# Product "4" of two pairs ahead of the first weight sums, and casts of weights bound behind snapshots on ScalarE

## The chip, the cores and the metric

The kernel runs on one core of a Trainium2 chip, as one program. The time is the device time of one execution, in microseconds (us); the median of several runs counts.

The engines of the core each run their own instructions in the order in which they were written down for them, and wait for one another by semaphores: TensorE (matmuls, called PE in the profile), VectorE (DVE), ScalarE (ACT), GpSimd (POOL) and SyncE (SP). SP, ScalarE and GpSimd issue DMAs; in this kernel GpSimd issues those that add to what is in memory already.

## The reference

A trunk of two layers works on 512 tokens of 1024 channels, with 16 learned tokens put ahead (528 in all). Each layer is a feed-forward block (FFN), a mixer (linear attention and softmax attention, merged by gates), and another FFN:

```
def swiglu(x, w_gate, w_up, w_down):
    return (jax.nn.silu(x @ w_gate) * (x @ w_up)) @ w_down
...
    for l in range(DEPTH):
        h = h + 0.5 * swiglu(rmsnorm(h, norm_gains[l, 0]),
                             ffn_w_gate[l, 0], ffn_w_up[l, 0], ffn_w_down[l, 0])
        h = h + mixer(rmsnorm(h, norm_gains[l, 1]), ...)
        h = h + 0.5 * swiglu(rmsnorm(h, norm_gains[l, 2]),
                             ffn_w_gate[l, 1], ffn_w_up[l, 1], ffn_w_down[l, 1])
    return rmsnorm(h, final_norm)[:, N_META:]
```

`rmsnorm` divides by the root of the mean square over the 1024 channels and multiplies by a gain. The inner width of an FFN is 2816, that is 22 tiles of 128, and everything is float32.

## The kernel before

**Layout.** The state `h` stays on chip, channels on the 128 partitions in 8 chunks (`KC`), 528 tokens along the row. A norm's gain is multiplied into the operand before the matmuls, and its factor 1/root(mean square), `rs`, afterwards, so the matmuls can begin before `rs` is known.

**Precision.** Every matmul runs in a rounded float32 and is done three times: operands and weights are split into a high and a low part, and high x high, high x low and low x high are added in PSUM. A block of weights, 128 x 1024 float32 (512 KB), is loaded into one of three buffers; ScalarE casts it to its high part (`whi`, L227) and VectorE subtracts that to get the low part (`wlo`, L228). Each kind has four buffers. `Weights.make` issues cast and subtraction in the order of the program's plan, some 3 or 4 blocks ahead of the product that uses them, and `Weights.fetch` the loads some 6 ahead.

**The FFN's gate and up projections.** 22 tiles make 11 pairs. For a pair the four products of a 2 x 2 block of weights with a 2 x 2 block of the operand (the tokens are cut in two halves, the channels in two halves) are replaced by seven, after Strassen and Winograd; their names are "1" to "7" and their order within a pair is mostly 1 2 5 6 7 4 3 or close to it. Products "1", "2" and "4" use the blocks 11, 12 and 22 of the weights as they are (`DIRECT`). Products "6", "7", "5" and "3" use sums of blocks, which no engine computes: s3 and s4 begin as the negative of a block on ScalarE (`negative`, L178), s1 and s2 as a load on SP, and a DMA on GpSimd's queue adds the other block in memory (`add`, L183). A product is 24 matmuls of 128 x 128 weights by up to 264 tokens (L517).

**Accumulators.** "1", "6", "7" and "4" of a pair add up in one PSUM tile (X), "5" and "3" in another (Z), "2" has its own (Y). Between two of them ScalarE copies the sum so far out of PSUM, the "snapshot" (L523): p1 after "1", q after "6", r after "7". The next product into that tile waits for the snapshot. VectorE adds these to the results `c`, and `hidden` makes silu(gate) x up of a tile, with `rs` multiplied in. `hidden(st, p, 1)` reads product "4"'s result in PSUM, so it takes the tile in two cuts.

**The order of steps.** `ffn_steps` writes an FFN's order out: `("P", pair, product)` and `("D", ...)` for pieces of the down projection, in three groups of 4, 4 and 3 pairs. The first group opens with 1 and 2 of pairs 0 and 1, then 6 and 5 of pair 0, 7, 4, 3, and so on. `weight_plan` makes the order of weights from the same list. After product "5" of pair 0 the kernel calls `norm.rs()`: the squares (L427) have been added by VectorE (L431); two pairs of matmuls with a constant sum them over the partitions (`means`, L399), ScalarE takes logarithm (L405) and exponential (L376) and a last square (L409), and VectorE makes a Newton step. These run at high priority. The scheduler of the framework puts each engine's instructions in order by priority and readiness; `after(x)` makes the instructions issued within it stay behind `x` on their engine, and `act` keeps ScalarE's functions in order in this way and notes the last of them in `prev_act`.

**The end.** The last FFN's down projection for the last three chunks (`LATE` = 5 to 7) is done for one half of the tokens and then for the other (`ending`). The final norm's factor is made for each half; `leave` multiplies two chunks of h by it (L1067) and sends them out (L1068). The first half leaves while the second half's chunks are computed.

## Time and profile before

| what | value |
| --- | --- |
| median of 3 runs | 2239.12 us (2236.11 to 2239.44) |
| the profiled execution | 2237.59 us |
| its span (first to last instruction) | 2235.8 us |
| TensorE matmul busy | 2197.9 us, 98% |
| VectorE / ScalarE / GpSimd busy | 68% / 54% / 7% |
| mean DMA rate over the span | 141 GB/s |

A line of a timeline has the start in us from the span's start, the duration, engine, source line, operation, output<-input by the program's names, shapes and a count; in brackets stands how long the engine had been idle before it and what ended that. "ss", "s2", "mm" are PSUM tiles, "xc" the FFN's operand, "t" a scratch tile. ACTq, POOLq and SPq stand for DMAs issued by these engines. Matmuls overlap: one is shown with 0.28 us, but the next begins 0.12 us after it.

### The profile page before, as it was taken

The page shows a single profiled execution, that of the slowest core. Times are in us where ns is not written, and L with a number is a line of the kernel's source. Part 1 is how long each engine was busy: PE and PEld are TensorE (multiplying, and loading weights), DVE is VectorE, ACT ScalarE, POOL GpSimd, SP SyncE. Part 2 cuts the span into 40 slices and gives each one's busy share as a digit, 9 for nine tenths or more (in the row PEclk, how much of TensorE's full clock was granted, in tenths as well). Part 3 has the DMA queues.
Part 4 walks back from the last instruction along what each step waited for, and adds up shares of the span by engine and source line. Part 5 has one row for each costly group of instructions (what it writes and reads, how often), then busy time and mean ns, then how long its engine had stood idle before and what let it go on. Part 6 is the DMA issues. An engine that isn't in the chain of part 4 may idle for free.

```text
span 2235.8 us, 39768 instructions
## 1 busy us (share of the span) xinstructions
PE 2197.9 (98%) x16506; PEld 2093.8 (94%) x16506; DVE 1521.6 (68%) x2415; ACT 1196.6 (54%) x1769; POOL 154.1 (7%) x180
## 2 busy tenths in 40 slices
PE   7999999999999999999999999999999999999998
PEld 6999999989999999999999999999788888989897
DVE  7657567586986676565696575675878767756566
ACT  7536355454785574453575363553457836636353
POOL 1111010000000010101011110100000001101010
PEclk9999999999999999999999999999999999999999
DMA  9769563212113485866667685632121136859671
GB/s 265 211 156 225 143 170 102 84 48 77 48 39 109 127 211 156 192 179 171 176 172 199 166 215 141 176 100 76 53 80 48 48 123 167 221 150 217 161 179 66
DMA packets 88612, 315.57 MB, mean 141 GB/s; under 512 B 9840, under 2 KB 12272, under 8 KB 88432
## 3 DMA queue, kind: packets, MB, share of 16 engines
q1 hardware_dynamic: 61136, 218.26, 29.1%
q0 software_dynamic: 25344, 92.29, 23.3%
q8 instruction: 129, 2.11, 0.4%
q10 hardware_dynamic: 1952, 2.50, 0.3%
q14 instruction: 51, 0.42, 0.1%
HBM read 264.77 MB, written 2.10 MB: 119 GB/s over the span
## 4 chain that ended last, share of the span: by engine, by line
PE 86%; DVE 6%; ACT 4%; DMA 3%; issue 1%; DVEq 0%; POOL 0%; ACTq 0%; POOLq 0%
PE ss L517 37%; PE ss L393 27%; PE mm L393 13%; PE sm L393 2%; DMA w<-win 2%; DVE wlo L228 1%; PE sm L894 1%; PE ss L869 1%; ACT whi L227 1%; ACT t L376 1%; PE sm L910 1%; PE sm L911 1%; PE ss L870 1%; PE ss L399 1%; PE sm L719 0%
## 5 line engine op out<-in xcount | busy, mean ns | idle before, releaser
L517 PE MATMUL ss<-xc,whi 128*128 128x264 f32 (+1 forms) x4928 | 903.9, 285 | 16.4 <-ACT whi L227 9.5
L517 PEld LDWEIGHTS ss<-xc,whi 128*128 128x128 f32 x4928 | 767.1, 189 | 20.0 <-ACT whi L227 9.7
L517 PE MATMUL ss<-xc,wlo 128*128 128x264 f32 (+1 forms) x2464 | 702.1, 285 | 2.7 <-DVE wlo L228 2.7
L393 PE MATMUL ss<-g,whi 128*128 128x264 f32 (+2 forms) x2692 | 495.4, 300 | 0.0
L517 PEld LDWEIGHTS ss<-xc,wlo 128*128 128x128 f32 x2464 | 466.0, 189 | 5.0 <-DVE wlo L228 4.7
L393 PEld LDWEIGHTS ss<-g,whi 128*128 128x128 f32 x2692 | 391.4, 188 | 16.2
L393 PE MATMUL mm<-x,whi 128*128 128x264 f32 (+1 forms) x1712 | 384.8, 315 | 0.0
L227 ACT CAST whi<-w 128x1024 fp32r<-128x1024 f32 (+1 forms) x221 | 230.7, 1046 | 259.8 <-PE ss L393 117.0
L227 ACT CAST whi<-raw 128x1024 fp32r<-128x1024 f32 x190 | 199.3, 1049 | 293.7 <-PE mm L393 97.9
L228 DVE TENSOR_TENSOR wlo<-w,whi 128x1024 fp32r<-128x1024 f32 (+1 forms) x221 | 267.7, 1218 | 107.8 <-ACT whi L227 106.0
L393 PE MATMUL ss<-g,wlo 128*128 128x264 f32 (+2 forms) x1346 | 312.2, 300 | 0.0
L228 DVE TENSOR_TENSOR wlo<-raw,whi 128x1024 fp32r<-128x1024 f32 x190 | 232.1, 1222 | 96.1 <-ACT whi L227 94.7
L393 PEld LDWEIGHTS mm<-x,whi 128*128 128x128 f32 x1712 | 278.4, 188 | 16.6 <-issue 1.0
L393 PE MATMUL mm<-x,wlo 128*128 128x264 f32 (+1 forms) x856 | 266.1, 315 | 0.0
L393 PEld LDWEIGHTS ss<-g,wlo 128*128 128x128 f32 x1346 | 215.7, 188 | 8.3
L228 DVE TENSOR_TENSOR wlo<-s,whi 128x1024 fp32r<-128x1024 f32 x88 | 107.6, 1223 | 97.1 <-ACT whi L227 97.0
L227 ACT CAST whi<-s 128x1024 fp32r<-128x1024 f32 x88 | 92.4, 1050 | 146.7 <-PE ss L517 127.1
L393 PEld LDWEIGHTS mm<-x,wlo 128*128 128x128 f32 x856 | 159.6, 188 | 8.5 <-issue 0.7
L483 DVE SCALAR_TENSOR_TENSOR t<-ss,rs 128x528 f32<-128x528 f32 (+1 forms) x93 | 64.5, 700 | 127.1 <-PE ss L393 127.0
L178 ACT ACTIVATE s<-w 128x1024 f32<-128x1024 f32 x88 | 93.2, 1060 | 75.5 <-DMA w<-win 41.3
L183 POOL DMA_DIRECT2D w<-win x44 | 38.9, 884 | 944.5 <-DMA w<-win 430.3
L523 ACT COPY snap<-ss 128x528 f32<-128x528 f32 (+1 forms) x132 | 77.1, 584 | 0.9 <-PE ss L517 0.9
(245 smaller groups left out, 2566.8 us busy)
## 6 DMA issues: line engine op xcount, KB each, us to landing
w<-win SPq DMA_DIRECT2D x219, 512.0 KB, 4.6
raw<-wts SPq DMA_DIRECT2D x190, 512.0 KB, 3.3
s<-win POOLq DMA_DIRECT2D x44, 512.0 KB, 7.3
w<-s POOLq DMA_DIRECT2D x44, 512.0 KB, 5.5
w<-win POOLq DMA_DIRECT2D x44, 512.0 KB, 7.0
s<-w POOLq DMA_DIRECT2D x44, 512.0 KB, 7.3
h<-xt SPq DMA_DIRECT2D x3, 528.0 KB, 6.4
out<-h ACTq DMA_DIRECT2D x4, 256.0 KB, 2.3
```

Of the source, the lines that this page charges most:

```text
L178: self.nc.scalar.activation(t, w, AF.Copy, scale=-1.0)
L183: self.nc.gpsimd.dma_start(t, src, accum_op=ALU.add)
L227: nc.scalar.copy(hi[:, cs], w[:, cs])
L228: nc.vector.tensor_tensor(lo[:, cs], w[:, cs], hi[:, cs].bitcast(F32), ALU.subtract)
L376: prev_act[0] = S.activation(*args, **kw).ins
L393: TE.matmul(acc.half[i][:width], lhs, rhs[:, acc.spans[i]], start=first, stop=last)
L399: TE.matmul(a, weights, x[:, hs], start=True, stop=True)
L483: V.scalar_tensor_tensor(cut(dst[rows]), pv[rows], -0.5 * f, cut(rs[rows]), ALU.mult, ALU.mult)
L517: TE.matmul(acc[:, j], a[:, j, k], b[:, at], start=bool(begin and k == 0 and i == 0), stop=k == len(x) - 1 and i == 2, skip_group_check=no ...
L523: S.copy(st[name], acc)
L869: TE.matmul(s[:n, i, :HF], lhs, kh[:, hs], start=True, stop=False)
L870: TE.matmul(s[:n, i, :HF], lhs, kl[:, hs], start=False, stop=True)
```

## The change

1. In the very first FFN (layer 0, first block) the order of steps opens with products 1, 2 of pairs 0 and 1 and then product "4" of both pairs; "6" and "5" of pair 0 follow. The loads of the plan move with them. Such an early "4" gets a PSUM tile of its own (W), ScalarE copies it to `c`, and after product "7" VectorE adds the snapshot r to it and calls `hidden` in one cut.
2. `Weights.make` issues its casts and the start of its sums under `issue_after(W.behind)`. `W.behind` is the last snapshot of pairs 0 and 1, in every FFN, and after `norm.rs()` it is the norm's last square, which is now issued through `act`. For later pairs it is None.
3. In `ending` all four `leave` of the first half come after the last chunk's add of the second half, and no longer between its chunks.

The arithmetic is the same but for the order in which r and product "4" are added in pairs 0 and 1 of the first FFN.

```diff
 DIRECT = {"1": "11", "2": "12", "4": "22"}
-def ffn_steps():
+def ffn_steps(opening):
     steps, pair = [], 0
...
         ahead = g == 0
         steps += [("P", p, c) for p in range(pair, pair + 1 + ahead) for c in "12"]
+        early4 = (0, 1) if opening and ahead else ()
+        steps += [("P", p, "4") for p in early4]
         steps += [("P", pair, c) for c in "65"]
         for i in range(n):
             p, more = pair + i, i + 1 < n
...
                 [[("D", g, 0, 0, 2 * n - 2)], [("D", g, 1, 0, 2 * n - 2)]]
             if ahead and i == 0:
                 early = [[], []]
-            steps += early[0] + [("P", p, "7")] + early[1] + [("P", p, "4"), ("P", p, "3")]
+            steps += early[0] + [("P", p, "7")] + early[1] + [("P", p, c) for c in "43" if c == "3" or p not in early4]
             if more:
                 steps += [("P", p + 1, "6"), ("P", p + 1, "5")]
         steps += [("D", g, m, 0, 2 * n - 2) for m in range(2, HELD)]
...
             plan.append(("tile", name, idx, k * P, col, width))
     def ffn(l, f):
-        for step in ffn_steps():
+        for step in ffn_steps((l, f) == (0, 0)):
             if step[0] == "P":
                 plan.append(("op", (l, f)) + step[1:])
             else:
...
         self.at = {load: i for i, load in enumerate(self.loads)}
         self.made, self.fetched, self.got, self.summed, self.raws = 0, 0, {}, {}, {}
         self.pos = 0
+        self.behind = None
     def dram(self, f, i, name):
         return self.win[((f[0] * 2 + f[1]) * NPAIR + i) * 4 + ("11", "12", "21", "22").index(name)]
...
             self.fetched += 1
     def make(self, upto):
+        with self.tc.issue_after(self.behind) if self.behind else nullcontext():
+            self.make_all(upto)
+    def make_all(self, upto):
         nc = self.nc
         while self.made < min(upto, len(self.loads)):
             self.fetch(self.made + 1)
...
         act(y, y, AF.Exp, scale=-0.5)
         if newton:
             u = slot("t", n=y.shape[-1])
-            S.activation(u, y, AF.Square)
+            act(u, y, AF.Square)
             V.scalar_tensor_tensor(cut(u), ms, EPS, cut(u), ALU.add, ALU.mult)
             V.scalar_tensor_tensor(y, u, 3.0, y, ALU.subtract, ALU.mult)
...
         def product_of_pair(p, product):
             kind = "s2" if p % 2 == 0 else "ss"
             st = made.setdefault(p, {})
+            apart = product == "4" and "r" not in st
             where, begin = {"1": ("X", 1), "6": ("X", 0), "7": ("X", 0), "4": ("X", 0), "2": ("Y", 1), "5": ("Z", 1),
                             "3": ("Z", 0)}[product]
+            if apart:
+                where, begin = "W", 1
             if begin:
                 st[where] = pair(kind == "s2")
             acc = st[where][:, :, :w]
...
             def snapshot(name):
                 t = slots["snap"].tile([P, T], F32, tag="snap", name=nm("snap"))[:, :n]
                 st[name] = v2(t)
-                S.copy(st[name], acc)
+                copied = S.copy(st[name], acc).ins
+                W.behind = copied if p < 2 else None
             if product == "1":
                 snapshot("p1")
...
                 V.tensor_tensor(st["c"][:, :, 0], st["p1"], acc, ALU.add)
             elif product == "6":
                 snapshot("q")
+            elif apart:
+                S.copy(st["c"][:, :, 2], acc)
+                st["apart"] = True
             elif product == "7":
                 snapshot("r")
                 V.tensor_tensor(st["c"][:, :, 3], st["r"], st["Z"][:, :, :w], ALU.add)
+                if "apart" in st:
+                    V.tensor_tensor(st["c"][:, :, 2], st["c"][:, :, 2], st["r"], ALU.add)
+                    hidden(st, p, 1)
             elif product == "4":
                 hidden(st, p, 1)
             elif product == "3":
...
             c = st["c"]
             t, u = [c[:, j, 2 * m : 2 * m + 2].rearrange("p q c -> p (q c)") for j in range(2)]
             x21 = st["X"][:, :, :w]
-            cuts = [(t, u, t, u, slice(0, n))] if m == 0 else \
+            cuts = [(t, u, t, u, slice(0, n))] if m == 0 or "apart" in st else \
                 [(t[:, :w], u[:, :w], x21[:, 0], x21[:, 1], slice(0, w)), (t[:, w:], u[:, w:], t[:, w:], u[:, w:], slice(w, n))]
             for td, _, ts, _, cs in cuts:
                 V.scalar_tensor_tensor(td, ts, -0.5, rs[:, cs], ALU.mult, ALU.mult)
...
             if g == len(GROUPS) - 1:
                 (done or finish_chunk)(m)
-        steps = ffn_steps()
+        steps = ffn_steps((l, f) == (0, 0))
         last_op = max(i for i, t in enumerate(steps) if t[0] == "P")
         for i, step in enumerate(steps):
             if step[0] == "P":
...
                 product_of_pair(*step[1:])
                 if step[1:] == (0, "5"):
                     rs = norm.rs()
+                    W.behind = prev_act[0]
                 if i == last_op:
                     close_pools(norm.pools)
                     following()
...
             product("ffn_w_down", acc, operand, len(w), only=i, w=w)
             t, sq[i] = slot("t")[:, hs[i]], slot("t")[:, hs[i]]
             V.scalar_tensor_tensor(t, acc.half[i], -0.25, rs[:, hs[i]], ALU.mult, ALU.mult)
-            V.tensor_tensor(h(c, hs[i]), h(c, hs[i]), t, ALU.add)
+            added = V.tensor_tensor(h(c, hs[i]), h(c, hs[i]), t, ALU.add).ins
             if c == KC - 1:
                 ms[i] = pair()[:, 0, : SEQ // 2]
                 TE.matmul(ms[i], o1024, fin.acc[:, hs[i]], start=True, stop=False)
...
             else:
                 TE.matmul(ms[i], o1024, sq[i], start=False, stop=True)
             gain(c, hs[i])
+            return added
         def factor(i):
             y[i], u = slot("t")[:, hs[i]], sq[i]
...
             chunk(0, c)
         factor(0)
         chunk(1, LATE)
-        leave(0, (0, 2))
         for c in range(LATE + 1, KC):
-            chunk(1, c)
-        leave(0, (4, 6))
+            added = chunk(1, c)
+        with after(added):
+            leave(0, (0, 2, 4, 6))
         factor(1)
         leave(1, (0, 2, 4, 6))
```

More of the change, by code (lines that the diff above doesn't have):

```diff
@@ L148, with __init__ @@
 class Weights:
-    def __init__(self, nc, raw, hi, lo, wts, win):
-        self.nc, self.raw, self.hi_pool, self.lo_pool, self.wts, self.win = nc, raw, hi, lo, wts, win
+    def __init__(self, tc, raw, hi, lo, wts, win):
+        nc = tc.nc
+        self.tc, self.nc, self.raw, self.hi_pool, self.lo_pool, self.wts, self.win = tc, nc, raw, hi, lo, wts, win
         self.long = self.short = None
@@ L277, in build @@
     small = pool("small", 4)
-    W = Weights(nc, pool("wraw", 3), pool("whi", 4), pool("wlo", 4), wts, win)
+    W = Weights(tc, pool("wraw", 3), pool("whi", 4), pool("wlo", 4), wts, win)
     pss = pool("pss", 2, bass.MemoryType.PSUM)
```

## The prediction

> **What bounds the kernel now.** I read the page first: its parts 1 and 5 for the engine that sets the time, then the windows of the start, then the timelines of the places where that engine stood idle.
>
> ```profile
> span 2235.8 us, 39768 instructions
> PE 2197.9 (98%) x16506; PEld 2093.8 (94%) x16506; DVE 1521.6 (68%) x2415; ACT 1196.6 (54%) x1769; POOL 154.1 (7%) x180
> ...
> L517 PE MATMUL ss<-xc,whi 128*128 128x264 f32 (+1 forms) x4928 | 903.9, 285 | 16.4 <-ACT whi L227 9.5
> L517 PE MATMUL ss<-xc,wlo 128*128 128x264 f32 (+1 forms) x2464 | 702.1, 285 | 2.7 <-DVE wlo L228 2.7
> ```
>
> TensorE is busy for 98% of the span. The number of matmuls doesn't change, so a change of order can only touch what is left: 2235.8 - 2197.9 = 37.9 us of idle time, and matmuls that ran at a lowered clock. Of the idle time 16.4 + 2.7 us stand ahead of the products of the gate and up projections (L517), where the edit works. The windows say where.
>
> ```profile
> 0.00:50.00 50.00, 34.60 (x208) 31.58 (x209) 36.93 (x63) 39.21 (x62) 8.25 (x13) 0.97 0.94 258
> 50.00:100.00 50.00, 50.00 (x413) 50.00 (x412) 36.79 (x47) 32.24 (x40) 6.95 (x8) 1.00 0.91 245
> ...
> 35.00:40.00 5.00, 3.75 (x28) 3.44 (x27) 4.69 (x6) 2.93 (x4) 1.73 (x2) 1.00 1.00 245
> 40.00:45.00 5.00, 1.54 (x9) 1.10 (x8) 2.09 (x4) 3.32 (x5) 0.88 (x1) 0.97 0.98 225
> 45.00:50.00 5.00, 5.00 (x32) 5.00 (x31) 3.23 (x5) 3.05 (x3) 0.88 (x1) 0.69 0.62 104
> ```
>
> The columns are the window, then TensorE matmul, weight load, VectorE, ScalarE and GpSimd busy with counts, then granted clock, DMA share and GB/s. In the first 50 us TensorE lacks 15.4 us; in the next 50 it lacks none, and 413 matmuls in 50 us give 0.121 us each, 2.9 us for a product of 24. So 35 to 50 us is the place to look at, and the DMA engines are full there until 45 us.
>
> ```profile
> 26.21 0.39 PE L517 MATMUL ss<-xc,wlo 128*128 128x264 f32 x1 [0.26 <-DVE wlo L228]
> 37.98 1.13 PE L399 MATMUL ss<-t,const 128*128 128x264 f32 x4 [1.25 <-issue]
> 42.55 0.52 PE L517 MATMUL ss<-xc,whi 128*128 128x264 f32 x2 [2.22 <-ACT whi L227]
> 44.31 0.51 PE L517 MATMUL ss<-xc,whi 128*128 128x264 f32 x2 [1.25 <-ACT snap L523]
> 46.16 0.64 PE L517 MATMUL ss<-xc,whi 128*128 128x264 f32 x2
> 46.82 0.64 PE L517 MATMUL ss<-xc,whi 128*128 128x264 f32 x2
> 48.13 0.41 PE L517 MATMUL ss<-xc,whi 128*128 128x264 f32 x2
> 48.51 0.40 PE L517 MATMUL ss<-xc,whi 128*128 128x264 f32 x2
> ...
> 24.53 0.59 ACT L523 COPY snap<-ss 128x528 f32<-128x528 f32 x1
> 35.41 0.64 ACT L427 ACTIVATE t<-h 128x528 f32<-128x528 f32 x1
> 41.45 1.04 ACT L227 CAST whi<-w 128x1024 fp32r<-128x1024 f32 x1 [3.52 <-DMA w<-s]
> 43.68 0.58 ACT L523 COPY snap<-ss 128x528 f32<-128x528 f32 x1
> ...
> 35.55 2.33 DVE L431 TENSOR_TENSOR t<-t,t 128x528 f32<-128x528 f32 x3
> 37.80 1.22 DVE L228 TENSOR_TENSOR wlo<-w,whi 128x1024 fp32r<-128x1024 f32 x1
> ```
>
> The reader is to see a ScalarE that runs in order: from 37.9 to 41.45 it waits with a cast for a sum of weights that a DMA adds in memory; the snapshot at 43.68, which frees TensorE's accumulator, is queued behind that cast. TensorE loses 2.22 + 1.25 us in these two stalls and 1.25 us before them in the means of the norm, which wait for VectorE's adds (ended at 35.55 + 2.33 = 37.88). Then three matmuls take 46.82 - 46.16 = 0.66 us in place of 48.51 - 48.13 = 0.38: the clock fell to 0.69, from 45 to 50 us, and 32 matmuls ran where 413 / 10 = 41 would have; with 0.121 us each that is 1.1 us, and some 0.5 more before 45 us, 1.6 in all (estimate).
>
> **The opening.** Before: 0.26 + 1.25 + 2.22 + 1.25 + 1.6 = 6.6 us lost from 26 to 50 us. After, two products "4" (2 x 2.9 us, weights loaded directly) come ahead of the first that needs a sum, so the sums have 5.8 us more to land. SP's queue changes with it: the direct block of pair 1 and a block of pair 2 pass the two loads that pair 1's sums begin with. What remains, from the order of instructions after and the durations above:
>
> The cast for the second product of pair 1 now stands behind a square and a snapshot. Their issue pitch on ScalarE is some 0.05 to 0.1 under the durations 0.64 and 0.59, so 1.1 us later; the low half follows, and the stall of 0.26 grows to about 0.9: +0.7 us against a start without it (I count 0.7 in all, since the product before it also ends later).
>
> The means still come early, three matmuls into product 7. VectorE's seven squares are added (2.33 / 3 = 0.78 us each) between the low halves of weights (1.22 each). They end between 38.8, with one low half in between, and 37.88 + 2 x 1.22 = 40.3 with two; TensorE arrives at 38.8 by my walk. So 0 to 1.5 us; I take 1.4, nearer to the upper end, since two low halves are ahead in the order.
>
> The wait of 41.45 goes: the cast of that sum is now due at 46.6 by the walk (six products from 26.9, the means' stall included), and the sum lands at 43.5 if its chain of load (SP) and addition (GpSimd's queue) is some 2 us later than before. Next is pair 2's first sum.
>
> ```profile
> 35.78 0.86 POOL L183 DMA_DIRECT2D w<-s  x1 [9.29 <-DVE t L431]
> 56.93 0.86 POOL L183 DMA_DIRECT2D w<-s  x1 [8.56 <-DMA w<-win]
> ...
> w<-s POOLq DMA_DIRECT2D x44, 512.0 KB, 5.5
> ```
>
> It was added from 56.93 for some 5.5 us, to 62.7. Its chain comes 2 to 3 us later, to about 66, cast and low half are ready by 68.3, and TensorE reaches it at 67.2 (71.4 before): 1.1 us; 0 if the chain isn't later, 2 if it is a us worse. The two new copies out of PSUM on ScalarE (about 0.59 each, the snapshot's row) and the two adds on VectorE cost nothing as long as the casts have the 5.8 us of cover; without it each is 0.6 us. Sum of the opening: 6.6 - 0.7 - 1.4 - 1.1 = 3.4 us gained; bounds -0.5 (second rival) to 5.9. I carry 3.3.
>
> **The other three first blocks.** Here only the rule on ScalarE acts: casts after the snapshots of pairs 0 and 1 and after the norm's last square.
>
> ```profile
> 1898.95 0.39 PE L517 MATMUL ss<-xc,wlo 128*128 128x256 f32 x1 [0.18 <-DVE wlo L228]
> 1902.96 0.50 PE L517 MATMUL ss<-xc,whi 128*128 128x256 f32 x2 [2.44 <-ACT snap L523]
> ...
> 1901.38 1.04 ACT L227 CAST whi<-w 128x1024 fp32r<-128x1024 f32 x1 [3.74 <-DMA w<-win]
> 1902.33 0.58 ACT L523 COPY snap<-ss 128x512 f32<-128x512 f32 x1
> ...
> 1158.54 1.13 PE L399 MATMUL ss<-t,const 128*128 128x264 f32 x4 [0.66 <-DVE t L431]
> ...
> 1900.00:1905.00 5.00, 2.56 (x22) 2.35 (x21) 2.25 (x3) 1.53 (x2) 0.00 (x0) 1.00 0.89 168
> 1905.00:1910.00 5.00, 5.00 (x45) 5.00 (x44) 2.62 (x5) 3.97 (x5) 1.52 (x2) 1.00 0.68 216
> ```
>
> In the last FFN (1903 us) the same picture as at 42 us: a cast waits 3.74 us for a sum, the snapshot behind it, TensorE 2.44 us. After, the snapshot goes first. TensorE then waits for it alone between product 7 and product 4: 0.58 us for the copy and some 0.1 to 0.2 to and from it, 0.65 to 0.85. The cast is due two products later, at 1907. Gone are 2.44 + 0.18, come are 0.65 to 0.85; a low half at 1885 us is tight (0 to 0.3): 1.5 to 2.0, and up to 2.9 if the bare wait is hidden as at other snapshots. I take 2.3. No clock is won here: it stayed at 1.00 after that single gap.
>
> In layer 0's second FFN (805 us) the bare wait also moves next to its product, without filler matmuls: 0.2 us lost (0 to 0.85). In layer 1's first FFN the means come 18 matmuls later (18 x 0.121 = 2.2 us): the 0.66 goes down to about 0.4; but the norm's logarithm then stands ahead of the snapshot, with two casts held behind: 1.0 for the wait and 0.35 for a low half, less 0.3: 1.0 us lost (0 to 2.3, one cast and one low half in full).
>
> **The tail.**
>
> ```profile
> 2223.65 0.68 DVE L1067 TENSOR_TENSOR h<-h,t 128x512 f32<-128x512 f32 x1
> 2224.58 0.68 DVE L1067 TENSOR_TENSOR h<-h,t 128x512 f32<-128x512 f32 x1
> 2225.18 0.42 DVE L1045 SCALAR_TENSOR_TENSOR t<-ss,rs 128x256 f32<-128x256 f32 x1
> ...
> 2228.78 0.42 DVE L1061 SCALAR_TENSOR_TENSOR t<-ss,t 128x256 f32<-128x256 f32 x1 [1.36 <-ACT t L1060]
> 2229.70 2.50 DVE L1067 TENSOR_TENSOR h<-h,t 128x512 f32<-128x512 f32 x4
> ```
>
> Two multiplies of the first half (0.68 each) stand before the last chunk's work at 2225.18. Behind its add they fill the time in which VectorE waits for the means (the 1.36): 1.3 us earlier, less 0.3 because the four in a row (2.50) end just after the factor is ready: 1.0 us gained (0.3 to 1.4). The four outputs of the first half now leave together, still ahead of the last four; if they collide, the gain is the 0.3.
>
> **Sum.** -3.3 + 0.2 + 1.0 - 2.3 - 1.0 = -5.4 us. The profiled execution took 2237.59 us (span 2235.8), so 2232.2 by its own time; the median of the runs is 1.5 us above it, and 2239.12 - 5.4 gives **2233.7**. Its own range, with the terms' ends, is 2230 to 2236.5. What a measurement of this kernel can tell from no change is about 0.2%, 4.5 us.
>
> **Rivals.**
>
> Rival 1, the sums come later by all that passes them: the gain goes back. Two blocks of 512 KB pass the loads of pair 1's sums; at the 258 GB/s of the first window each is 2.0 us, 4.1 together where I took 2. For it: DMA share 1.00 and 0.98 from 35 to 45 us. Against it: the share falls to 0.62 at 45, so there is room to catch up. Then the sum due at 46.6 lands at 45.4, its low half is ready at 47.7 or later: 1.1 us, and if that comes with the means' stall the clock goes too, as at 44.31: 1.6. Pair 2's sums, later by the same 2.1 us while TensorE is later by the 1.1, add about 0.9. The whole: -5.4 + 1.1 + 1.6 + 0.9 = -1.8, which is 2237.3. The Trainium skill, page "DMA: Bandwidth & Descriptors", section "Issuing engines are not separate DMA queues", says that queues of several engines share the same 16 DMA engines and that spreading transfers over them doesn't add bandwidth. By that rule what is pulled ahead on SP is paid by GpSimd's additions, which is this rival; the share of 1.00 agrees, no row yet shows the order in which the two queues are served.
>
> Rival 2, slower: ScalarE's casts wait for TensorE's snapshots, and TensorE for the casts. The place is the start of the four first FFN blocks, two pairs each, eight places; the price is one cast and one low half in full, 1.04 + 1.22 = 2.27 us, where the weight held back is the next that TensorE needs. I count 0.7 + 0.2 + 1.0 for it. From three more places in full (5.4 / 2.27 = 2.4) the change loses; with five, 2233.7 + 11.3 = 2245.0. For it: the low halves are already late at 26.21 and 1898.95. Against it: four buffers for each half let the casts run ahead by about a product or more.
>
> Rival 3, the wait at 1903 only changes its place: the sum lands at 1901.38 whatever the order, and where the product that needs it also moves up, 2.3 us are not won: 2236.0.
>
> A rule of the page "TensorE: Matmul & The Clock Gate" of the Trainium skill, Part 1, is that the clock goes to half after an idle window of about 3.4 us and back after a busy one. The 3.5 us of 42.55 and 44.31 together (0.69 after them) and the single 2.44 (1.00) agree with it. By it a stall of 1.4 us alone costs no clock, which is the sum above.
>
> **Chances.** Forecast 0.50; rival 1 0.20; rival 2 0.15; rival 3 0.15. Faster by over 0.2% (under 2234.6) holds most of the forecast's case and a little of rivals 1 and 3: 0.50. Rival 2 is 0.15 slower; the rest, 0.35, is within 0.2%. The range takes the forecast's ends, rivals 1 and 3 and the mild part of rival 2: 2229.5 to 2241.0.
>
> **What would show it.** Right: no wait on a sum ahead of a cast at 41 and 1901 us with the snapshot behind it; TensorE's window of 45 to 50 at clock 1.00; its idle time in the first 50 us 2 to 4 us under 15.4; the last multiplies at about 2228.7 less the gain so far. Wrong: a new gap of over 2 us ahead of a product 6 or 5 between 45 and 75 us (rival 1), several gaps released by casts or low halves at the starts of FFN blocks (rival 2), or 2.4 us still lost near 1903 (rival 3).

## The result, and the profile after

The changed kernel takes 2251.80 us (median of 6 runs, 2247.80 to 2254.03) against 2239.34 us before (6 runs): a ratio of 1.0053, 95% interval 1.0039 to 1.0066. It is 12.5 us slower where 5.4 us of gain were forecast. The profiled execution has a span of 2252.3 us, 16.5 above that of before; it is the slowest of its six runs, while the profile of before lies under its median, so some 4 us of the 16.5 are the choice of executions.

The page of the changed kernel (its L529 is L517 of before, L535 is L523, L236 is L227, L237 is L228, L183 is L178 and L188 is L183):

```profile
span 2252.3 us, 39746 instructions
PE 2203.9 (98%) x16506; PEld 2098.9 (93%) x16506; DVE 1522.0 (68%) x2413; ACT 1196.0 (53%) x1771; POOL 154.5 (7%) x180
...
L529 PE MATMUL ss<-xc,whi 128*128 128x264 f32 (+1 forms) x4928 | 909.9, 286 | 26.9 <-ACT snap L535 14.1
L529 PE MATMUL ss<-xc,wlo 128*128 128x264 f32 (+1 forms) x2464 | 703.6, 286 | 4.0 <-DVE wlo L237 4.0
```

Idle time ahead of the products grew from 16.4 to 26.9 us, and its main releaser is no longer a cast but the snapshot (14.1). TensorE's busy time grew by 6.0 us with the same matmuls, which is a lowered clock (its mean over the span is 0.995 in place of 0.998). The timeline of the changed kernel has the places: first TensorE's gaps, then ScalarE beside the stalls at 1215 and 1957 us, then windows around the stalls:

```profile
40.46 0.91 PE L408 MATMUL ss<-t,const 128*128 128x264 f32 x3 [1.07 <-ACT snap L535]
69.89 0.51 PE L529 MATMUL ss<-xc,whi 128*128 128x264 f32 x2 [2.21 <-ACT whi L236]
71.14 0.39 PE L529 MATMUL ss<-xc,wlo 128*128 128x264 f32 x1 [0.75 <-DVE wlo L237]
91.19 0.81 PE L529 MATMUL ss<-xc,whi 128*128 128x264 f32 x2 [3.87 <-ACT snap L535]
1215.30 0.54 PE L529 MATMUL ss<-xc,whi 128*128 128x264 f32 x2 [3.76 <-ACT snap L535]
1912.79 0.51 PE L529 MATMUL ss<-xc,whi 128*128 128x256 f32 x2 [0.67 <-ACT snap L535]
1956.81 0.80 PE L529 MATMUL ss<-xc,whi 128*128 128x256 f32 x2 [4.05 <-ACT snap L535]
...
1213.70 1.04 ACT L236 CAST whi<-w 128x1024 fp32r<-128x1024 f32 x1 [4.50 <-DMA w<-s]
1214.65 0.59 ACT L535 COPY snap<-ss 128x528 f32<-128x528 f32 x1
1955.23 1.04 ACT L236 CAST whi<-w 128x1024 fp32r<-128x1024 f32 x1 [4.65 <-DMA w<-s]
1956.18 0.58 ACT L535 COPY snap<-ss 128x512 f32<-128x512 f32 x1
...
70.00:75.00 5.00, 4.25 (x23) 4.04 (x24) 5.00 (x7) 4.74 (x6) 1.19 (x2) 0.72 0.80 138
90.00:95.00 5.00, 3.81 (x17) 3.81 (x18) 4.02 (x5) 2.19 (x3) 0.87 (x1) 0.50 0.65 129
1215.00:1220.00 5.00, 4.70 (x26) 4.70 (x27) 3.63 (x5) 1.36 (x3) 0.13 (x1) 0.66 0.96 224
1955.00:1960.00 5.00, 3.19 (x16) 3.19 (x17) 2.85 (x4) 2.26 (x3) 0.87 (x1) 0.66 1.04 256
```

The stalls of 42, 44 and 1903 us are gone, as intended. But the same figure, a cast that waits for a sum with the snapshot queued behind it, now stands some 45 us further on, at pair 3 of three FFNs (91, 1215 and 1957 us), and there no cast is bound. Each costs 3.8 to 4.1 us, and the granted clock in the 5 us around or after it is 0.50 to 0.66. (At 40.46 the bracket names the snapshot, but VectorE's last add of the squares ended at 40.36, and it is what the means wait for.)

How much later the same matmul, counted from the start, begins in the changed kernel, stage by stage (one profiled execution each, so the rows carry the scatter told of below, the first three most):

| stage | shift there, us | forecast, us |
| --- | --- | --- |
| opening, to the 16th product | -4.5 | -4.5 |
| first product 6 and 5 of pair 2 (70 us) | +5.0 | +1.1 |
| pair 3 of the first FFN (91 us) | +6.3 | 0 |
| layer 0, second FFN | +0.3 | +0.2 |
| layer 1, first FFN, its start | +1.4 | +1.0 |
| the same, pair 3 (1215 us) | +5.5 | 0 |
| layer 1, second FFN, its start | -2.5 | -2.3 |
| the same, pair 3 (1957 us) | +5.6 | 0 |
| tail, to the last multiplies | -1.0 | -1.0 |

From the last multiplies to the end of the span the changed kernel takes 0.5 us more than the kernel before, so 0.5 of the 1.0 us reaches the end.

### The profile page after: what moved, and what is told of

It is laid out like the page before. It is cut to its first block, busy times and chain, and to the rows that moved or that the text cites. A ratio compares the mean times of both kernels' runs of the same rounds, so it can differ in the third digit from the quotient of the medians.

```text
span 2252.3 us, 39746 instructions
## 1 busy us (share of the span) xinstructions
PE 2203.9 (98%) x16506; PEld 2098.9 (93%) x16506; DVE 1522.0 (68%) x2413; ACT 1196.0 (53%) x1771; POOL 154.5 (7%) x180
## 4 chain that ended last, share of the span: by engine, by line
PE 82%; DVE 6%; DMA 6%; ACT 4%; issue 2%; POOL 0%; SPq 0%; DVEq 0%; POOLq 0%; ACTq 0%
PE ss L529 33%; PE ss L402 26%; PE mm L402 13%; DMA w<-win 3%; PE sm L402 2%; DMA w<-s 2%; DMA s<-win 2%; DVE wlo L237 1%; PE sm L914 1%; PE ss L889 1%; ACT whi L236 1%; PE sm L930 1%; PE ss L408 1%; PE sm L931 1%; PE ss L890 1%
## 5 line engine op out<-in xcount | busy, mean ns | idle before, releaser
L529 PE MATMUL ss<-xc,whi 128*128 128x264 f32 (+1 forms) x4928 | 909.9, 286 | 26.9 <-ACT snap L535 14.1
L529 PEld LDWEIGHTS ss<-xc,whi 128*128 128x128 f32 x4928 | 771.2, 190 | 31.8 <-ACT snap L535 15.3
L529 PE MATMUL ss<-xc,wlo 128*128 128x264 f32 (+1 forms) x2464 | 703.6, 286 | 4.0 <-DVE wlo L237 4.0
L529 PEld LDWEIGHTS ss<-xc,wlo 128*128 128x128 f32 x2464 | 468.3, 190 | 6.0 <-DVE wlo L237 5.9
L236 ACT CAST whi<-w 128x1024 fp32r<-128x1024 f32 (+1 forms) x221 | 230.2, 1046 | 266.1 <-PE ss L402 118.0
L237 DVE TENSOR_TENSOR wlo<-w,whi 128x1024 fp32r<-128x1024 f32 (+1 forms) x221 | 267.7, 1218 | 127.5 <-ACT whi L236 126.0
L236 ACT CAST whi<-raw 128x1024 fp32r<-128x1024 f32 x190 | 199.3, 1049 | 290.1 <-PE mm L402 97.8
L237 DVE TENSOR_TENSOR wlo<-raw,whi 128x1024 fp32r<-128x1024 f32 x190 | 232.1, 1222 | 95.2 <-ACT whi L236 93.8
L402 PEld LDWEIGHTS mm<-x,whi 128*128 128x128 f32 x1712 | 278.4, 188 | 16.5 <-issue 1.0
L237 DVE TENSOR_TENSOR wlo<-s,whi 128x1024 fp32r<-128x1024 f32 x88 | 107.6, 1222 | 89.6 <-ACT whi L236 89.6
L236 ACT CAST whi<-s 128x1024 fp32r<-128x1024 f32 x88 | 92.4, 1050 | 131.7 <-PE ss L529 113.5
L183 ACT ACTIVATE s<-w 128x1024 f32<-128x1024 f32 x88 | 93.2, 1059 | 71.4 <-DMA w<-win 40.9
L188 POOL DMA_DIRECT2D w<-win x44 | 39.7, 903 | 938.2 <-DVE wlo L237 390.6
L535 ACT COPY snap<-ss 128x528 f32<-128x528 f32 (+1 forms) x132 | 77.2, 585 | 20.0 <-PE ss L529 20.0
```

What stands on the lines that cost most here:

```text
L183: self.nc.scalar.activation(t, w, AF.Copy, scale=-1.0)
L188: self.nc.gpsimd.dma_start(t, src, accum_op=ALU.add)
L236: nc.scalar.copy(hi[:, cs], w[:, cs])
L237: nc.vector.tensor_tensor(lo[:, cs], w[:, cs], hi[:, cs].bitcast(F32), ALU.subtract)
L402: TE.matmul(acc.half[i][:width], lhs, rhs[:, acc.spans[i]], start=first, stop=last)
L529: TE.matmul(acc[:, j], a[:, j, k], b[:, at], start=bool(begin and k == 0 and i == 0), stop=k == len(x) - 1 and i == 2, skip_group_check=no ...
```

## The experiments

Theory A in the expectations is that the bound casts hold back the sums of later pairs; theory B, that the new order of the opening crowds out the loads. "Binding" is part 2 of the change. A ratio is against the kernel before, measured beside each kernel (medians of 2239.91 to 2240.87 us).

### The parts alone

**Opening and tail without the binding.**

```diff
-                W.behind = copied if p < 2 else None
+                W.behind = None
...
-                    W.behind = prev_act[0]
```

> Parts 1 and 3 of the change alone: the new opening and the moved first-half outputs, and no cast is bound behind anything. Theory A (the bound casts give their weight buffers back late, so later loads and sums slip, and two pairs on a late sum's cast holds a snapshot): without the binding the stalls of 3.8 to 4.1 us at 91, 1215 and 1957 us are gone, the opening gains 3 to 6 us and the tail 1.0: 2232 to 2236 against 2239. Theory B (the pulled-forward direct blocks crowd out the loads of the sums, my rival 1): the opening stays 6.8 us slower whatever the binding, minus 1.0 for the tail: 2244 to 2246.

2239.30 us against 2240.87, ratio 0.9997 (0.9988 to 1.0005). The loss is gone, the gain did not come. Timeline of this kernel:

```profile
53.89 0.51 PE L529 MATMUL ss<-xc,whi 128*128 128x264 f32 x2 [3.18 <-DVE c L551]
1905.87 0.50 PE L529 MATMUL ss<-xc,whi 128*128 128x256 f32 x2 [2.12 <-ACT snap L535]
...
45.40 1.05 ACT L236 CAST whi<-w 128x1024 fp32r<-128x1024 f32 x1 [4.25 <-DMA w<-s]
46.35 0.69 ACT L414 ACTIVATE rs<-ss,eps 128x528 f32<-128x528 f32 x1
```

No stall near 91, 1215 or 1957 us. But without the binding the norm's logarithm (46.35) waits behind the cast of a late sum (45.40), and 3.18 us are lost at 53.89; the opening ends 1.1 us later than before.

**The binding alone.** The tail is the old one, too.

```diff
-        early4 = (0, 1) if opening and ahead else ()
+        early4 = ()
```

> Part 2 alone: the binding of ScalarE's casts in all four FFNs, the old opening and the old tail. Theory A: all of the loss is here: layer 0's second FFN +0.4, layer 1's first +6.7, its second +3.1 as in the changed kernel, and the opening somewhere from -2 (the stalls at 42 and 44 us go) to +5 (they come back two pairs later): 2247 to 2254. Theory B: the opening's loss is the reorder's, so the first 440 us are no slower than before, and the other FFNs give at most their local waits: 2240 to 2244 if the later stalls follow from the first FFN's shift, which nothing passes on.

2252.95 us, ratio 1.0059 (1.0048 to 1.0071): the whole loss. The stalls are the changed kernel's (the third is smaller, 2.45 us at 1958.65):

```profile
91.36 0.81 PE L529 MATMUL ss<-xc,whi 128*128 128x264 f32 x2 [4.22 <-ACT snap L535]
1217.83 0.81 PE L529 MATMUL ss<-xc,whi 128*128 128x264 f32 x2 [5.40 <-ACT snap L535]
```

So theory B falls as the cause of the loss: the old opening has the stall at 91 us too as soon as the casts are bound.

**The tail alone.**

```diff
-        leave(0, (0, 2))
         for c in range(LATE + 1, KC):
-            chunk(1, c)
-        leave(0, (4, 6))
+            added = chunk(1, c)
+        with after(added):
+            leave(0, (0, 2, 4, 6))
```

> Part 3 alone: the first half's four multiplies and outputs behind the last chunk's add. In the changed kernel the step from the first half's factor to the second half's was 1.0 us shorter than before, so both theories say -1.0 us: 2238 against 2239, at the edge of what five rounds can tell. If that 1.0 came with the other parts, 0.

2239.32 us, ratio 0.9997 (0.9988 to 1.0006). The step of 1.0 us to the last multiplies is in the trace of every kernel with the new tail; what follows takes 3.6 us in some of them and 4.1 in others, so 0.5 to 1.0 us of it reaches the end. The times can't show it.

### Which of the bound casts

**The norm's last square binds nothing.**

```diff
-                    W.behind = prev_act[0]
+                    W.behind = None
```

> The whole change, but after product 5 of pair 0 the casts are bound to nothing (not to the norm's last square), until the snapshot after product 7. Theory A in its sharp form (in layer 1's first FFN the cast of pair 1's first sum, 6 us late behind logarithm, snapshot and square, holds the buffer that pair 2's sum needs): the stall of 3.76 at 1215 and the clock after it go, and that FFN comes back from +6.7 to under +1.5; the first FFN from +6.8 to 0 to +3: 2238 to 2245 against 2252 for the changed kernel. If the snapshots alone make the loss, it stays at 2250 to 2253.

2246.18 us, ratio 1.0032 (1.0019 to 1.0045), just over the expected 2238 to 2245: about half of the loss is gone. There is no stall near 1215 any more; what is left at pair 3 is smaller, 1.38 us at 91, 1.90 at 853 (told of with the clock below), and

```profile
1950.30 0.50 PE L529 MATMUL ss<-xc,whi 128*128 128x256 f32 x2 [1.76 <-ACT snap L535]
```

**Only casts of blocks that need no sum are bound.**

```diff
-        with self.tc.issue_after(self.behind) if self.behind else nullcontext():
-            self.make_all(upto)
+        self.make_all(upto)
...
-                nc.scalar.copy(hi[:, cs], w[:, cs])
+                with self.tc.issue_after(self.behind) if self.behind and not isinstance(load, int) and load[2] in DIRECT else nullcontext():
+                    nc.scalar.copy(hi[:, cs], w[:, cs])
```

> The whole change, but only the casts of blocks that need no sum are bound; casts of sums and the negatives that begin them are free. Theory A: the sums' buffers come back in time, so the stalls of 3.8 to 4.1 us near pair 3 are gone in the second layer's FFNs, and the waits that the binding was to remove return (2.1 to 2.4 near 1905): 2237 to 2242. If the bound casts of direct blocks (three load buffers) make the sums late, it stays at 2247 to 2254.

2243.76 us, ratio 1.0018 (1.0008 to 1.0028), some 2 us over the expected 2237 to 2242. The stalls near 91 and 1957 are gone, the one near 1215 is 1.19 us (at 1207.76). Waits that the binding was to remove are back (2.29 us at 50, 2.06 at 1163, 0.87 at 1904). In layer 1's first FFN most of the loss only moved: 4.5 us at its start and 1.4 at pair 3, together 5.9, against 1.4 and 5.5 in the changed kernel. So the stalls at pair 3 need the bound casts of sums or the bound negatives, which are both free here; the next run parts them.

**The negatives free, all casts bound.** In the changed kernel:

```diff
-        with self.tc.issue_after(self.behind) if self.behind else nullcontext():
-            self.make_all(upto)
+        self.make_all(upto)
...
-                nc.scalar.copy(hi[:, cs], w[:, cs])
+                with self.tc.issue_after(self.behind) if self.behind else nullcontext():
+                    nc.scalar.copy(hi[:, cs], w[:, cs])
```

> The whole change, but the negatives on ScalarE that begin the sums s3 and s4 are not bound; all casts are. In the order of instructions this moves one of them, in the opening (pair 2's first sum begins two instructions earlier), and leaves the other FFNs as they are. Theory A: the opening gains up to 6 us (a stall of 3.8 at 91 us smaller or gone), layer 1's stalls near 1215 and 1957 stay: 2246 to 2251. If the negatives are the whole cause everywhere: 2238 to 2242.

2247.27 us, ratio 1.0030 (1.0019 to 1.0040): over 40% of the loss is gone. The traces show more than the one move that was expected. In three FFNs, all but layer 1's first, a negative now stands ahead of the snapshot and of casts that wait for sums; in the last FFN, after the change and then with the negatives free:

```profile
1917.63 1.06 ACT L183 ACTIVATE s<-w 128x1024 f32<-128x1024 f32 x1
```

```profile
1907.24 1.06 ACT L183 ACTIVATE s<-w 128x1024 f32<-128x1024 f32 x1 [1.87 <-DVE wlo L237]
```

There the stall at pair 3 falls from 4.05 to 0.58 us (at 1949.38), and the one at 71 us in the first FFN is gone. In layer 1's first FFN, where the order on ScalarE is the changed kernel's, the stall stays (3.97 us at 1211), and in the first FFN it stays too (4.41 at 86.81). So, as far as one profile tells, the late stall of the last FFN needs the negatives' own binding, and in layer 1's first the bound casts are enough.

**Two casts held, in one FFN.** The kernel before, where only in layer 1's first FFN the casts of pair 0's s4 and of pair 1's s2 are bound.

```diff
+BIND = ((1, 0),)
...
+                with self.tc.issue_after(self.behind) if self.behind and not isinstance(load, int) and load[0] in BIND and load[1:] in ((0, "3"), (1, "6")) else nullcontext():
```

> The kernel before, and in layer 1's first FFN alone two casts of sums (product 3 of pair 0, product 6 of pair 1) are bound behind the norm's last square or the snapshot after it. Theory A: these two casts come some 3 us later, and this alone makes the loads and additions of the sums up to pair 3 slip by 3 to 8 us, so that a stall of 1 to 4 us appears near 1208 us that the kernel before hasn't: 2241 to 2247. If only the bound casts of many blocks together did it: no stall near 1208, 2239 to 2241.

2242.33 us, ratio 1.0011 (1.0002 to 1.0020). The additions up to pair 3 slipped by 1 to 3.5 us against the matmuls at the FFN's start, but no stall came near 1208; only the snapshot between products 7 and 4 is paid (1.14 us at 1168.31). This half of the forecast of theory A missed, though the total lies within it: two casts make the slip, not the stall. The kernel before has some 3 us of slack there (the sum for pair 3 landed at 1197.04 and was cast at 1200.09).

### By which link

In the changed kernel's first FFN of layer 1 (the matmuls are 7.1 us later than before at its start) ScalarE, VectorE and GpSimd's queue show the slip; before, then after:

```profile
1159.44 1.22 DVE L228 TENSOR_TENSOR wlo<-s,whi 128x1024 fp32r<-128x1024 f32 x1
1161.13 1.05 ACT L178 ACTIVATE s<-w 128x1024 f32<-128x1024 f32 x1
1178.99 1.06 ACT L178 ACTIVATE s<-w 128x1024 f32<-128x1024 f32 x1 [0.80 <-DVE wlo L228]
1173.75 0.89 POOL L183 DMA_DIRECT2D w<-s  x1 [10.29 <-DVE c L550]
1192.06 0.89 POOL L183 DMA_DIRECT2D w<-s  x1 [9.74 <-DVE wlo L228]
```

```profile
1170.96 1.03 ACT L236 CAST whi<-s 128x1024 fp32r<-128x1024 f32 x1
1171.89 2.94 ACT L236 CAST whi<-w 128x1024 fp32r<-128x1024 f32 x3
1172.45 1.22 DVE L237 TENSOR_TENSOR wlo<-s,whi 128x1024 fp32r<-128x1024 f32 x1
1174.74 1.05 ACT L183 ACTIVATE s<-w 128x1024 f32<-128x1024 f32 x1
1196.37 1.05 ACT L236 CAST whi<-w 128x1024 fp32r<-128x1024 f32 x1 [3.81 <-DMA w<-win]
1197.33 1.05 ACT L183 ACTIVATE s<-w 128x1024 f32<-128x1024 f32 x1
1185.10 0.89 POOL L188 DMA_DIRECT2D w<-s  x1 [8.04 <-DVE wlo L237]
1207.42 0.89 POOL L188 DMA_DIRECT2D w<-s  x1 [7.77 <-DMA w<-win]
```

The cast at 1170.96 is that of pair 0's s4; its buffer is the one in which pair 2's s3 begins, and it is free when the low half is made too, at 1159.44 + 1.22 = 1160.66 before and 1172.45 + 1.22 = 1173.67 after. So pair 2's negative moves from 1161.13 to 1174.74, 6.5 us more than the matmuls; 5.9 of them are the buffer, and the rest is its place behind the bound casts. Pair 2's sums come late; a cast that waits 3.81 us for one of them (no longer bound) holds up the next negative, pair 3's, which moves from 1178.99 to 1197.33. The addition for pair 3 goes from 1192.06 to 1207.42: 15.4 us, where the matmuls are 8.4 later. The 7.0 us between them, less the 3 us of slack, come near the stall of 3.76. With the norm's square free the same negative is 4.9 us late and the addition for pair 3 only 1.9, within the slack: no stall. Two runs gave the buffers of the sums one more each.

**A third buffer for s1 and s2.**

```diff
-        pools = open_pools("left", wsa=3, wsb=2)
+        pools = open_pools("left", wsa=3, wsb=3)
-    slots = {n: pool("s_" + n, b) for n, b in dict(g=16, t=6, rs=2).items()}
+    slots = {n: pool("s_" + n, b) for n, b in dict(g=16, t=5, rs=1).items()}
```

> The whole change with a third buffer for the sums s1 and s2 (before: two); the memory comes from one scratch tile (five in place of six) and one tile of the norm's factor (one in place of two). Theory A (a bound cast holds the sum's buffer, and the next sum can't be loaded): with a third buffer the load of pair 2's and pair 3's sums no longer waits for the bound cast, and the stalls of 3.8 to 4.1 us near 91, 1215 and 1957 us shrink by at least half, unless the three buffers of s3 and s4 hold them up alone: 2239 to 2246, plus what the smaller pools cost. If the buffers have no part in it: stalls as in the changed kernel and 2250 or more.

2255.74 us, ratio 1.0074 (1.0061 to 1.0088). The first two stalls grew: 7.53 us at 96.62, 5.20 at 1221.28. There these buffers are not the link. The last is smaller, 1.00 at 1960, so in the last FFN they may be a part of it.

**A fourth buffer for s3 and s4** (`wsa=4, wsb=2`, memory as above).

> The whole change with a fourth buffer for the sums s3 and s4 in place of three (memory as in the run with more room: five scratch tiles, one factor tile). If the bound cast of pair 0's s4 holds the buffer in which pair 2's s3 begins, the negative now stands ahead of the bound casts on ScalarE, pair 2's and pair 3's sums land 4 to 10 us earlier, and the stalls near 91, 1215 and 1957 us fall to under 1.5 us: 2236 to 2244. If the load buffers or the DMA engines set it, the stalls stay and 2250 to 2256 comes out.

2284.03 us, ratio 1.0192 (1.0173 to 1.0210). The total went far the other way, but the trace answers the question for the second layer. In layer 1's first FFN the negative stands ahead of the bound casts again, directly after the snapshot:

```profile
91.93 0.51 PE L529 MATMUL ss<-xc,whi 128*128 128x264 f32 x2 [1.36 <-ACT snap L535]
205.51 0.81 PE L529 MATMUL ss<-xc,whi 128*128 128x264 f32 x2 [4.90 <-ACT snap L535]
1342.37 0.81 PE L529 MATMUL ss<-xc,whi 128*128 128x264 f32 x2 [4.46 <-ACT snap L535]
...
1185.19 1.06 ACT L183 ACTIVATE s<-w 128x1024 f32<-128x1024 f32 x1
```

The stalls at pair 3 of the second layer's FFNs are gone, and its first FFN's pairs 0 to 3 lose 1.3 us in place of 6.9. In the first FFN of all the answer is open: the stall near 91 falls from 3.87 to 1.36 us, but the one ahead of it grows from 2.21 (at 69.89) to 3.84 (at 72.66). New stalls of 1 to 6 us stand in the later groups of all four FFNs (205, 975, 1342, 2087 us), where nothing is bound. The run with a third s1 and s2 buffer and the same small pools has none there, so the small pools are not their cause; the order in which the additions are queued differs there, and whether that makes them was not tried.

**The negatives on VectorE**, three buffers.

```diff
-        self.nc.scalar.activation(t, w, AF.Copy, scale=-1.0)
+        self.nc.vector.tensor_scalar_mul(t, w, -1.0)
```

> The whole change with the negatives that begin s3 and s4 on VectorE in place of ScalarE, three buffers as before. If the place in ScalarE's queue makes them late (behind bound casts, and behind a cast that waits for a late sum), the stalls near 91, 1215 and 1957 us fall to under 1.5 us: 2236 to 2244. If the buffer does, the negative still waits for the low half of the bound cast on VectorE and, in the queue there, holds other work: 2247 to 2256.

2276.59 us, ratio 1.0156 (1.0139 to 1.0173), outside both forecasts. The stalls grew: 11.54 us at 96, 4.97 at 863, 6.44 at 1236, 6.37 at 1980. But the run does not part the buffer from the queue. In layer 1's first FFN the low half that frees the buffer, and then the negative:

```profile
1185.92 1.22 DVE L237 TENSOR_TENSOR wlo<-s,whi 128x1024 fp32r<-128x1024 f32 x1
1193.25 0.69 DVE L183 TENSOR_SCALAR s<-w 128x1024 f32<-128x1024 f32 x1
```

The buffer is free at 1187.14, and the negative comes 6.1 us after that, behind other low halves and VectorE's own work. One queue has taken the other's place. So it is the run with the fourth buffer that shows the buffers of s3 and s4, held by bound casts, as the start of the slip in layer 1's first FFN; that the queue behind a late cast then makes it grow is read from the trace and not shown by a run of its own.

### A narrow binding

In the first and the last FFN, only the casts for products "6" and "5" of pair 1 are bound. The idea is that they wait for their sums in any case, so that holding them behind the norm's square or the snapshot gives no buffer back later.

```diff
+BIND = ((0, 0), (1, 1))
...
+                with self.tc.issue_after(self.behind) if self.behind and not isinstance(load, int) and load[0] in BIND and load[1] == 1 and load[2] in "65" else nullcontext():
```

**With the new opening and the new tail.**

> New opening and new tail, and of the binding only what frees a snapshot: the casts of the sums for products 6 and 5 of pair 1, in the first FFN and in the last one. Theory A (the loss comes from casts that give the sums' buffers back late): these two casts wait for their DMA anyway, so nothing is given back later, and no stall near pair 3 (90, 1215, 1955 us). The last FFN keeps the 2.5 us that the binding won there (stall at 1906 gone), the tail its 1.0, and the opening the 4.5 us up to its 16th product, of which the next sum may take 1 to 4 back: 2233 to 2238 against 2240. Theory C (any cast bound behind a snapshot lets the sums slip): 2243 to 2252.

2239.55 us, ratio 0.9997 (0.9987 to 1.0007), over the expected 2233 to 2238. No stall near 1215 or 1957, 2.5 us won in the last FFN; in the first a late sum costs 2.34 us at 84.90, at the product of pair 3 where the changed kernel lost 3.87.

**With the old opening and the new tail.**

```diff
-        early4 = (0, 1) if opening and ahead else ()
+        early4 = ()
```

> The same narrow binding and the new tail with the old opening. Theory A: at 42 us the norm's chain no longer waits behind the cast that waits for a sum, so up to 3 us of the stalls at 42 and 44 us go, and 2.5 us of the last FFN, and 1.0 of the tail: 2233 to 2238. If the opening is bound by the DMA engines, what is won at 42 us comes back as a later sum at 70: 2236 to 2238. Theory C: 2243 and above.

2233.96 us against 2240.28, ratio 0.9971 (0.9960 to 0.9981): faster than both kernels.

```profile
42.77 0.51 PE L530 MATMUL ss<-xc,whi 128*128 128x264 f32 x2 [2.22 <-ACT snap L536]
1898.86 0.51 PE L530 MATMUL ss<-xc,whi 128*128 128x256 f32 x2 [0.68 <-ACT snap L536]
...
39.38 0.70 ACT L415 ACTIVATE rs<-ss,eps 128x528 f32<-128x528 f32 x1 [1.22 <-PE ss L409]
42.14 0.58 ACT L536 COPY snap<-ss 128x528 f32<-128x528 f32 x1
42.62 1.05 ACT L237 CAST whi<-w 128x1024 fp32r<-128x1024 f32 x1
```

The logarithm no longer waits for the sum (39.38; before, it came behind the cast of 41.45), one stall of 2.22 us is left of the two, the clock from 45 to 50 us is 0.79 in place of 0.69, and the last FFN's 2.44 us is 0.68.

**The narrow binding in all four FFNs.**

```diff
-BIND = ((0, 0), (1, 1))
+BIND = ((0, 0), (0, 1), (1, 0), (1, 1))
```

> The old opening, the new tail and the narrow binding (casts of the sums for products 6 and 5 of pair 1) in all four FFNs instead of two. In layer 0's second FFN the narrow binding without it left a stall of 1.6 us near 806; theory A says it can be had there too: 0 to 1.5 us better than with two FFNs, but in layer 1's first FFN the cast for product 6 is held a few us as in the run that holds two casts, and may cost 0 to 4 us: 2231 to 2238.

2233.60 us, ratio 0.9974 (0.9963 to 0.9985), not to be told from two FFNs. In layer 0's second FFN it wins, in layer 1's first it pays 1.00 us for the bare snapshot at 1159.

## Why the prediction was wrong

**Right by its own steps.** The opening up to the 16th product (-4.5; the means' wait 1.07 where 1.4 stood), the second FFN of layer 0 (+0.3 against +0.2), the start of layer 1's first FFN (+1.4 against +1.0), the start of the last FFN (-2.5 against -2.3, with the bare snapshot at 0.67 us) and the tail (-1.0). That the matmuls waiting at 1903 us need the sum two products later held too; rival 3 did not come. The closeness of these numbers is in part luck: in the run with two casts held, layer 0's second FFN and the last one are the kernel before's, and there the shift still changes by 1.3 and 1.4 us.

**The step that failed** is what follows from the sentence "Here only the rule on ScalarE acts": only the starts of the blocks are priced, and from pair 2 on (in the first FFN behind pair 2's first sum) the cost is put at nothing, without a reason. It priced what a held cast does to the product that needs it, and not what it does to the buffer that it frees; nor that the negatives, which begin later sums, are held too. A term for pair 3 was missing in three FFNs: 6.3 + 5.5 + 5.6 = 17.4 us of the span, of which 3.87 + 3.76 + 4.05 = 11.7 is idle time and most of the rest the clock. The experiments show the binding as its cause (1.0059 alone, 0.9997 without it). In layer 1's first FFN the bound casts are enough, with the buffers of s3 and s4 as the first link (6.9 us lost, 1.3 with a fourth buffer); in the last FFN the stall needs the bound negative too (4.05 us, 0.58 with it free). Which of the two begins the stall at 91 us stays open.

**A term that was mis-sized** is pair 2's first sum: 1.1 us expected, 2.21 + 0.75 of idle time and a clock of 0.72, 5.0 us in all. Its upper bound of 2 left the clock out. The scatter of the opening is as large.

**The rivals.** Rival 2 named the binding as what could lose, with a chance of 0.15 and 2245 us, but with a wrong price: one cast and one low half at the held place. The price is paid two pairs later and is the sum's lateness plus the clock. Rival 1 had late sums, but from transfers that pass them. Its sign came, a gap of 2.21 us at 69.89; but of the profiles of the new opening with the negatives on ScalarE, the four with bound negatives have it (2.2 to 4.4 us) and the four with free ones have none, though the plan of the loads is the same. So the bound negative makes it. The run of opening and tail without the binding has none of the stalls at pair 3. With 0.9997 it does show that the opening's gain of 3.3 us is not to be had by the order alone: late sums take it back, at 53.89 there and at 84.90 with the narrow binding. The DMA engines are full ahead of both (share 1.03 from 40 to 45 and 1.04 from 80 to 85 us); that this makes the sums late is likely and was not tried.

**The clock.** Around the changed kernel's gaps of 3.76 to 4.05 us the granted clock was 0.50 to 0.66, which cost some 1.6 to 2.4 us beyond each gap. Shorter gaps went either way. After 2.44 us at 1903 in the kernel before, the clock stayed at 1.00; in the run with two casts held, whose last FFN is the same, it was 0.74 from 1910 to 1915 us after a gap of 2.39. The stall of 2.22 us at 42 us that the narrow binding leaves cost clock with two FFNs bound (0.79 from 45 to 50 us) and none with four (1.00). After 2.45 us with the binding alone the clock fell a microsecond later, and after 1.90 us with the square free it fell at once (three matmuls again take 0.66 us):

```profile
1958.65 0.51 PE L529 MATMUL ss<-xc,whi 128*128 128x256 f32 x2 [2.45 <-ACT snap L535]
...
1960.00:1965.00 5.00, 5.00 (x32) 5.00 (x32) 2.41 (x4) 2.00 (x2) 0.00 (x0) 0.68 0.82 192
```

```profile
853.02 0.59 PE L529 MATMUL ss<-xc,whi 128*128 128x264 f32 x2 [1.90 <-ACT snap L535]
...
853.63 0.64 PE L529 MATMUL ss<-xc,whi 128*128 128x264 f32 x2
...
854.29 0.64 PE L529 MATMUL ss<-xc,whi 128*128 128x264 f32 x2
```

The Trainium skill's page "TensorE: Matmul & The Clock Gate", Part 1, gives an idle window of about 3.4 us, and calls the window free-running. The long gaps agree with it; as a safe bound for a gap the 3.4 us does not hold here (1.90 us at 853). The prediction took it to say that a stall of 1.4 us costs no clock: the 1.07 us stall at 40.46 did not, but 2.21 and 0.75 us close together at 70 us did.

## What to carry to other kernels

When an order edge holds an instruction back, follow what that instruction frees, not only what it feeds: the buffer, the load that waits for it, and the next user of that buffer, until the slack is known to take it up. Do the same for instructions behind the edge that start a chain of their own, as the negatives do here. A walk that stops where the instruction order is the same again can miss the whole effect. And where an in-order engine stalls behind one operation that waits for a transfer, bind that one operation only: two casts in each of the two FFNs that stalled, with the new tail, won 6 us in the medians, where binding all casts of the first pairs lost 12.

## What the runs showed that was not expected

The opening scatters from execution to execution by as much as the change was to win. (Other stages do so by less, as the 1.3 and 1.4 us above show.) With the same order of instructions in the opening, pair 2's first sum was ready by 63.3 us in the profile of before and at 68.75 in that of the tail alone:

```profile
63.32 1.05 ACT L227 CAST whi<-w 128x1024 fp32r<-128x1024 f32 x1 [1.27 <-PE ss L517]
```

```profile
68.75 1.04 ACT L236 CAST whi<-w 128x1024 fp32r<-128x1024 f32 x1 [6.09 <-DMA w<-s]
70.35 0.81 PE L529 MATMUL ss<-xc,whi 128*128 128x264 f32 x2 [3.40 <-ACT snap L535]
```

In the second a stall of 3.40 us follows, and the rest of the program is 5.7 us later; the two medians are the same within the interval. A single profile of the first 75 us can't price an edit there. Part of what the narrow binding wins in the medians (6.3 us, against some 3.6 between the profiled spans) may be that its runs lack such stalls (2231 to 2235 us for seven runs); only one of them has a trace, so that stays open.
